# Fronts and w2 by Strassen's algorithm: joining copies of the fronts on ScalarE, the first summed tile of w2 in v's buffers, sums of h spread wider

## The chip, the cores and the metric

The kernel runs on one core of one Trainium2 chip. The metric is the device time of one execution in microseconds, the median of several runs; lower is better. The engines are called PE (matrix products), ACT (ScalarE), DVE (VectorE), POOL (GpSimd) and SP (SyncE, which here issues DMAs).

## The reference

A trunk of two layers works on 256 tokens (SEQ) of width 1024 (D_MODEL); the hidden width of a feed-forward part (FFN) is 2816 (D_FF). All of it is float32.

```python
def _swiglu(x, w1, w3, w2):
    return (jax.nn.silu(x @ w1) * (x @ w3)) @ w2

for l in range(DEPTH):                       # DEPTH = 2
    h = _swiglu(x, ffn_w1[l, 0], ffn_w3[l, 0], ffn_w2[l, 0])
    x = _layernorm(ALPHA * x + 0.5 * h, ln_g[l, 0], ln_b[l, 0])
    h = _mixer(x, l, ...)                    # gated unit and differential attention
    x = _layernorm(ALPHA * x + h, ln_g[l, 1], ln_b[l, 1])
    h = _swiglu(x, ffn_w1[l, 1], ffn_w3[l, 1], ffn_w2[l, 1])
    x = _layernorm(ALPHA * x + 0.5 * h, ln_g[l, 2], ln_b[l, 2])
```

The change concerns the four `_swiglu` calls. In order of time they are FFN 1 (0 to 189 us of the profiled execution), FFN 2 (421 to 607), FFN 3 (607 to 786) and FFN 4 (1018 to 1210); a mixer lies between FFN 1 and 2 and between FFN 3 and 4.

## The kernel before

**Products in three parts.** A float32 product is made of three faster ones: each operand is split into a high half and a low half, and PE adds hi·hi, lo·hi and hi·lo. Weights come from memory as tiles of 1 MB (`raw`, 128x2048; four buffers). For each half of such a tile, 128x1024, ACT copies the high half (`whi`) and DVE subtracts it from the tile, which gives the low half (`wlo`). Streamed tiles are split at L188 and L190 (`stream`), Strassen tiles at L234 and L236 (`split`). `hhi` and `hlo` are the halves of the hidden activations h. High and low halves have eight buffers each, so ACT and DVE can be at most a few tiles ahead of PE.

**The front of an FFN.** The tokens are two blocks t of 128. The columns of w1 and w3 are taken in five blocks of 512 (n = 0, 1, 2, 4 straight, by `rows_b`; n = 3 by Strassen's seven products, `seven`, one of which is fed in between two units of the others), and a rest of narrow columns by `gemm_a2`, whose low halves run at L289 and whose banks ACT empties at L290. For each block and t, Silu of one bank times the other gives a 128x512 tile, which must be turned (transposed) before it can be the left operand of w2. `transposed` does this in three steps: `parted` (L205) writes the two 16-bit halves of every number apart, a DMA on SP's queue transposes them (`moved`, L211; it stands behind the last load issued), and `joined` (L216) interleaves the halves again, with two copies for a tile. An FFN has ten such tiles, so 20 joining copies, and they run on POOL. The joined tile is then split into h_hi and h_lo.

**w2.** `gemm_seven` takes a 1024x1024 part of w2 by seven products P1 to P7 (L358) and the other columns and blocks straight (L387), some of these between two products (`between`). P1 uses r1 = w11, P2 w21, P3 r1 + r2 with r2 = w12, P4 r1 + r3 with r3 = w22, P5 r3, P6 r2 + w22, P7 r1 + w21 (the first two sums and their successors are made in place). `plus` (L342) adds two tiles on DVE; `gather` adds a tile from memory by an accumulating DMA that POOL issues. r2 and r3 are loaded into `spare`: two buffers that held x in the front. The left operands are blocks of h and four sums of them (`sums_of_h`, `strassen_sums`, L809). `ln.fold` (L584) adds a product's bank into the tokens.

**What sets the order.** PE's order is the order of the program text. The other engines are ordered by the priorities with which the text issues: `beside` starts a side task, which yields its delays in beats; a beat is the time of twelve matmuls. `front(n, wait)` gives the beats from the end of the product to the joining copies, through `turned`. Each engine then works its list strictly in order, and waits at the head of it. The buffers of tag "val" (called v's here: the mixer's value tiles) hold planes of blocks n = 0 and 2 in the fronts.

Of the kernel before, what the change touches and what calls it, by code (L numbers as in the profile page):

```python
# [11 lines left out]
F32 = mybir.dt.float32  # L12
# [4 lines left out]
AF = mybir.ActivationFunctionType  # L17
# [37 lines left out]
def trunk(ctx, tc, x, xT, w13a, w13b, w2, wb, wqk, wu, wg, wgr, wbr, wbrr, wo, gateb, gatebr, sgug, sgub, sguwT, sgubias, lam, diffg,  # L55
# [81 lines left out]
    def beside(task, delay):  # L137
        tasks.append([clock[0] + delay, task])
# [55 lines left out]
    def planes(v):  # L194
        return v.bitcast(U16).rearrange("p (w c) -> p w c", w=2)

    def numbers(v):
        return v.bitcast(U16).rearrange("p (c w) -> p w c", w=2)
# [14 lines left out]

    def joined(src, out, eng):
        for w in range(2):
            eng.tensor_copy(out=numbers(out)[:, w], in_=planes(src)[:, w])  # L216

    def transposed(src, out, via, lead, first, second, eng, to=None, by=None):

# [142 lines left out]
    def gemm_seven(src, xh, xl, sums, spare, ln, done):  # L362

        q = [[bank(), bank()], [side_bank(), bank()]]
        bx, bz = side_bank(), q[1][0]
        (w11, w21), (w12, w22) = ([s[:, o : o + CH] for o in (0, CH)] for s in src)

        def rest(c):
            for k in range(8, FT, 4):
                nk = min(4, FT - k)
                for j, piece in enumerate(stream(src[c][:, k * 512 : (k + nk) * 512], nk * 512)):
                    yield k + 2 * j, piece  # L380

        def rows(t, c, k0, piece, o=0, n=512):
            for j in range(2):
                k = k0 + j
                hi, lo = (w[:, j * 512 + o : j * 512 + o + n] for w in piece)
                for m, (y, x) in enumerate(((hi, xh), (lo, xh), (hi, xl))):
                    PE.matmul(q[c][t][:, :n] if o == 0 else more[:, :n], x(k, t), y,  # L387
                              start=k == 8 and m == 0 and (c, t) != (1, 0), stop=k == FT - 1 and m == 2, skip_group_check=True)
            beat(n / 1024)

        def block(t, k0):
            return tuple(lambda k, f=f: f(k0 + k, t) for f in (xh, xl))

        a11, a12, a22 = block(0, 0), block(0, 4), block(1, 4)
        first = rest(0)

        def between():
            k, piece = next(first)
            for t in range(NT):
                rows(t, 0, k, piece)  # L400

        r1 = fetch(w11)
        product(bx, a11, pieces(r1), True, False)
        ln.fold(0, 0, bx, ALU.add, True)
        between()
        product(q[0][0], a12, pieces(fetch(w21)), False, False)
        r2, r3 = (fetch(w, raw=v) for w, v in zip((w12, w22), spare))
        between()
        product(bz, sums[0], pieces(plus(r1, r2)), True, False)
        ln.fold(1, 1, bz, ALU.add, True)  # L410
        between()
        product(bx, sums[1], pieces(plus(r1, r3)), False, False)
        ln.fold(0, 1, bx, ALU.subtract, True)
        between()
        product(bz, sums[3], pieces(r3), False, False)
        between()
        product(bx, sums[2], pieces(gather(r2, w22)), False, False)
        ln.fold(1, 1, bx, ALU.subtract, False)
        between()
        product(bx, a22, pieces(gather(r1, w21)), False, True)  # L420
        ln.fold(1, 0, bx, ALU.add, True)
        between()
        for t in range(NT):
            done(t, q[0][t], 0, 512)
        held = list(rest(1))
        cuts = ((0, 512),), (((0, 256), (256, 256)) if ln.last else ((0, 512),))
        for t in range(NT):
            for o, n in cuts[t]:
                more = bank() if o else None
                for k, piece in held:  # L430
                    rows(t, 1, k, piece, o, n)
                done(t, (more if o else q[1][t])[:, :n], 512 + o, n)
# [289 lines left out]
    def ffn(l, f, i, norm, last=False):  # L722
# [42 lines left out]
        def turned(n, t, s, p, wait):  # L765
            lead = 3.5 if n == 0 and norm else 0
            to = slots("held", 2)[0] if n < 2 else p
            yield from transposed(s, p, s, lead, wait - lead, 0.6, G, to, A if n else G)
            yield 0.6
            if n < 2:  # L770
                held[n, t] = to
            if (n, t) != (0, 1):
                split(h_hi[2 * n + t], h_lo[2 * n + t], to, after=(silu[0], added[0]))
            if (n, t) == (1, 1):
                yield 1
                yield from sums_of_h()
# [3 lines left out]
        def sums_of_h():  # L780

            h11, h21, h12, h22 = (held[v] for v in ((0, 0), (0, 1), (1, 0), (1, 1)))
            made = [[h_hi[1], h_lo[1]]] + [[slots("sum", 2, F32R)[0] for _ in range(2)] for _ in range(2)]
            made.append([tmp.tile([P, 512], F32R, tag="side", name=name("sum"), bufs=4) for _ in range(2)])
            yield from strassen_sums(sums, made, h11, h21, h12, h22)

        def sums_of_x():

# [13 lines left out]
            made = [[home(v) for v in w] for w in (("main", "side"), ("side", "main"), ("main", "slot"), ("side", "slot"))]  # L802
            yield from strassen_sums(x_sums, made, t11, t21, t12, t22)

        def strassen_sums(to, made, v11, v21, v12, v22):
            to[:] = [tuple(lambda k, v=v: v[:, k * P : (k + 1) * P] for v in m) for m in made]
            for n, (out, a, b, op) in ((0, (v22, v21, v22, ALU.subtract)), (2, (v21, v11, v21, ALU.subtract)),
                                       (1, (v11, v22, v11, ALU.subtract)), (3, (v12, v12, v11, ALU.add))):
                V.tensor_tensor(out=out, in0=a, in1=b, op=op)  # L809
                if n in (2, 3):  # L810
                    yield 1
            for n, out in ((0, v22), (2, v21), (1, v11), (3, v12)):
                split(*made[n], out)
                yield 1

        def seven(src, x_sums):

# [23 lines left out]
            product(bz, x_sums[3], pieces(r3), False, True)  # L841
            V.tensor_tensor(out=v0, in0=bz, in1=v0, op=ALU.subtract)
            V.tensor_tensor(out=g0, in0=g0, in1=v0, op=ALU.mult)
            beside(turned(3, 0, g0, v0, 8.3), 0)
            yield
            product(bx, x_sums[2], pieces(r2), False, False)
            V.tensor_tensor(out=v1, in0=v1, in1=bx, op=ALU.subtract)
# [1 line left out]
            product(bx, x22, pieces(r1), False, True)  # L849
            A.activation(g1, bx, AF.Silu)  # L850
            V.tensor_tensor(out=g1, in0=g1, in1=v1, op=ALU.mult)
            beside(turned(3, 1, g1, v1, 6.3), 0)
            yield

        def w13(n):
# [1 line left out]

        x_sums = []
        if norm is None:
            gemm_first(w13(0), both_done(0, (10.3, 10.3)))  # L860
            beside(sums_of_x(), 1)
        else:
            gemm_b2(w13(0), xh, xl, both_done(0, (13.3, 10.3)), norm=norm)
            beside(sums_of_x(), 5)
        products, unit = seven(w13(3), x_sums), 0
        for n in (1, 2, NB - 1):
            ps = [[bank() for _ in range(2)] for _ in range(NT)]
            ready = front(n, (9.3, 8.3))
            for c in range(2):
                for m in range(2):  # L870
                    got = stream(w13(n)[m][:, c * CH : (c + 1) * CH])
# [8 lines left out]
        for j in range(FA, FT - 4, 2):  # L880
            for m, z in gemm_a2([w13a[l, f, j - FA + m] for m in range(2)], both, lambda m: t512("silu")):
# [1 line left out]
                silu[0] = A.activation(s, s, AF.Silu).ins  # L883
                V.tensor_tensor(out=s, in0=s, in1=z[:, T:], op=ALU.mult)
                split(*(v[-1][:, (j - FA + m) * T : (j - FA + m + 1) * T] for v in (h_hi, h_lo)), s)
        spare = [xs.tile([P, 4, 512], F32, tag="x", name=name("spare")).rearrange("p k c -> p (k c)") for _ in range(2)]
        ln = Norm(l, i, 2.0 * ALPHA, 4.0 * EPS, s[:, :1], last)

        def done(t, p, c, n):
# [396 lines left out]
```

## Time and profile before

| what | value |
|---|---|
| median of 3 runs | 1212.04 us (1209.83 to 1216.02) |
| the profiled execution | 1212.16 us, its span 1210.1 us |
| PE busy | 1187.0 us, 98% of the span |
| DVE busy | 1033.7 us, 85% |
| ACT busy | 798.6 us, 66% |
| POOL busy | 333.2 us, 28% |
| granted PE clock, mean | 0.999 |
| bytes moved | 281.39 MB, 233 GB/s |

A row of the timeline has the start and the duration in us, the engine, the line, the operation with output and inputs, and in brackets the idle time of the engine ahead of it and what ended that. The span is the profiled execution on the chip; the device time holds 2.06 us more.

### The profile page before, as it was taken

To read this page: it belongs to the slowest core of one execution; us is meant where nothing else is said; L and a number is where in the kernel's file an instruction comes from. 1 tells how busy PE (TensorE), PEld (TensorE's weight loads), DVE (VectorE), ACT (ScalarE), POOL (GpSimd) and SP (SyncE) were. 2 spreads that over 40 slices of the span, in tenths; PEclk is the share of its full clock that TensorE was granted. 3 is DMA by queue.
4 is the path that set the end of the run, shared out by engine and by line. 5 is a ranking of instruction groups with operands and counts; after the bars stand their busy time and mean duration, and the time that the engine had idled before them with its cause. 6 is when DMAs were issued, how large, how long until landed. Compare 5 with 4: busy or idle time off the path is not lost.

```text
span 1210.1 us, 16672 instructions
## 1 busy us (share of the span) xinstructions
PE 1187.0 (98%) x5771; PEld 993.5 (82%) x5771; DVE 1033.7 (85%) x1548; ACT 798.6 (66%) x1372; POOL 333.2 (28%) x414
## 2 busy tenths in 40 slices
PE   9998999999999999999999999999999999999998
PEld 7886788888888888887888887888888888888876
DVE  6799889797688988989898999888966989989895
ACT  6478558668955665775565765676788556667760
POOL 2243301246420222413022413003564012133120
PEclk9999999999999999999999999999999999999999
DMA  9996885767865659879759779676676754896880
GB/s 351 289 300 213 241 311 186 265 206 209 248 206 181 223 185 270 214 241 265 258 192 268 210 254 274 237 260 244 209 206 204 252 188 152 259 257 205 285 246 35
DMA packets 130084, 281.39 MB, mean 233 GB/s; under 512 B 89120, under 2 KB 90192, under 8 KB 104912
## 3 DMA queue, kind: packets, MB, share of 16 engines
q1 hardware_dynamic: 120816, 248.80, 62.3%
q0 software_dynamic: 8752, 31.00, 11.1%
q8 instruction: 45, 0.74, 0.2%
q10 hardware_dynamic: 432, 0.52, 0.1%
q14 instruction: 39, 0.32, 0.1%
HBM read 254.35 MB, written 1.05 MB: 211 GB/s over the span
## 4 chain that ended last, share of the span: by engine, by line
PE 84%; DVE 9%; DMA 5%; issue 2%; ACT 1%; SPq 0%; DVEq 0%; ACTq 0%
PE bank L270 42%; PE bank L282 15%; PE bank L289 7%; PE sbank L358 7%; PE bank L387 5%; PE sbank L387 3%; DVE wlo L190 2%; DMA spare<-in_w 2%; DVE wlo L236 2%; DVE raw L342 2%; DMA raw<-in_w 1%; PE bank L491 1%; DVE held L809 1%; PE sbank L945 1%; DVE hlo L236 1%
## 5 line engine op out<-in xcount | busy, mean ns | idle before, releaser
L190 DVE TENSOR_TENSOR wlo<-raw,whi 128x1024 fp32r<-128x1024 f32 (+1 forms) x374 | 428.2, 1176 | 43.0 <-ACT whi L188 30.3
L188 ACT ACTIVATE whi<-raw 128x1024 fp32r<-128x1024 f32 (+1 forms) x378 | 351.4, 959 | 148.3 <-PE bank L270 39.4
L270 PE MATMUL bank<-whi,x 128*128 128x512 f32 x1224 | 386.3, 390 | 0.0
L270 PEld LDWEIGHTS bank<-whi,x 128*128 128x128 f32 x1224 | 229.8, 188 | 47.5
L270 PE MATMUL bank<-wlo,x 128*128 128x512 f32 x612 | 239.0, 391 | 5.7 <-DVE wlo L190 5.6
L282 PE MATMUL bank<-x,whi 128*128 128x512 f32 x640 | 153.3, 391 | 0.0
L270 PEld LDWEIGHTS bank<-wlo,x 128*128 128x128 f32 x612 | 114.9, 188 | 31.7 <-DVE wlo L190 8.6
L282 PEld LDWEIGHTS bank<-x,whi 128*128 128x128 f32 x640 | 118.2, 188 | 23.8
L236 DVE TENSOR_TENSOR wlo<-raw,whi 128x1024 fp32r<-128x1024 f32 (+1 forms) x96 | 113.9, 1205 | 18.1 <-ACT whi L234 7.5
L234 ACT ACTIVATE whi<-raw 128x1024 fp32r<-128x1024 f32 (+1 forms) x96 | 92.9, 982 | 38.3 <-DVE raw L342 18.6
L289 PEld LDWEIGHTS bank<-x,wlo 128*128 128x128 f32 x640 | 81.4, 191 | 2.9
L289 PE MATMUL bank<-x,wlo 128*128 128x256 f32 x640 | 82.6, 283 | 0.0
L387 PE MATMUL bank<-whi,hhi 128*128 128x512 f32 (+1 forms) x182 | 68.2, 375 | 0.0
L387 PE MATMUL bank<-wlo,hhi 128*128 128x512 f32 (+1 forms) x182 | 67.9, 373 | 0.0
L387 PE MATMUL bank<-whi,hlo 128*128 128x512 f32 (+1 forms) x182 | 67.9, 373 | 0.0
L216 POOL COPY planes<-planes 128x512 uint16<-128x512 uint16 x32 | 40.7, 1329 | 55.2 <-DMA planes<-planes 30.4
L921 POOL TENSOR_TENSOR swap<-swap,sin_t 128x512 f32<-128x512 f32 x16 | 27.9, 1742 | 98.9 <-DMA swap<-z 80.5
L698 POOL COPY nvia<-ntwo 128x256 uint16<-128x256 uint16 x20 | 10.0, 548 | 153.0 <-DMA ntwo<-nvia 139.7
L290 ACT ACTIVATE r<-bank 128x256 f32<-128x256 f32 x96 | 34.8, 372 | 24.5 <-PE bank L289 24.5
L205 ACT ACTIVATE planes<-planes 128x512 uint16<-128x512 uint16 x48 | 27.4, 619 | 31.0 <-DVE planes L751 31.0
L216 POOL COPY held<-planes 128x512 uint16<-128x512 uint16 x32 | 46.2, 1645 | 5.6 <-DMA planes<-planes 5.6
L216 POOL COPY seven<-seven 128x512 uint16<-128x512 uint16 x16 | 20.9, 1353 | 77.4 <-DMA seven<-seven 38.2
(285 smaller groups left out, 2210.1 us busy)
## 6 DMA issues: line engine op xcount, KB each, us to landing
raw<-in_w13b SPq DMA_DIRECT2D x68, 1024.0 KB, 6.6
raw<-in_w SPq DMA_DIRECT2D x32, 1024.0 KB, 6.3
raw<-in_wb SPq DMA_DIRECT2D x16, 1024.0 KB, 6.7
raw<-in_wqk SPq DMA_DIRECT2D x16, 1024.0 KB, 5.9
r<-in_w13b SPq DMA_DIRECT2D x16, 512.0 KB, 8.0
raw<-in_w13a SPq DMA_DIRECT2D x8, 1024.0 KB, 4.8
spare<-in_w SPq DMA_DIRECT2D x8, 1024.0 KB, 6.8
raw<-in_wgr SPq DMA_DIRECT2D x8, 1024.0 KB, 5.2
```

The source lines that it names most:

```text
L188: A.activation(h, r, AF.Copy)
L190: eng.tensor_tensor(out=w, in0=r, in1=h.bitcast(F32), op=ALU.subtract)
L216: eng.tensor_copy(out=numbers(out)[:, w], in_=planes(src)[:, w])
L234: a = A.activation(hi, src, AF.Copy).ins
L236: return a, eng.tensor_tensor(out=lo, in0=src, in1=hi.bitcast(F32), op=ALU.subtract).ins
L270: PE.matmul(ps, xx, w, start=start and n == 0, stop=stop and n == 2)
L282: PE.matmul(b[-1], hi[:, k * P : (k + 1) * P], xc(k), start=k == 0, stop=False)
L289: PE.matmul(b[n][:, :T], lo[:, k * P : (k + 1) * P], xc(k)[:, :T], start=False, stop=k == KT - 1)
L290: emptied[0] = A.activation(r[:, s], b[n][:, T:], AF.Copy, scale=scale).ins
L358: PE.matmul(ps, x[o](k), y, start=start and k == n == 0, stop=stop and k == 3 and n == 2, skip_group_check=True)
L387: PE.matmul(q[c][t][:, :n] if o == 0 else more[:, :n], x(k, t), y, start=k == 8 and m == 0 and (c, t) != (1, 0), stop=k == FT - 1 and m == ...
L921: turned_by[0] = G.tensor_tensor(out=s3, in0=s3, in1=s, op=ALU.mult).ins
```

## The change

- **Joining copies.** `joined` can run on ACT, as activations with Copy, and the fronts' `turned` uses that: 80 copies leave POOL. The delay ahead of the copies grows from 0.6 to 2.6 beats behind the transposing DMA, and the beats ahead of that DMA, given to `front` and to the two tiles of `seven`, shrink by 2 or 2.3, so the DMA is issued earlier and the copies come at about the same beat. For block n = 4 the beats ahead of the DMA stay, and its copies come two beats later.
- **First summed tile of w2.** r2 goes into two buffers of tag "val", r3 into one x buffer. r2 is loaded and added to r1 before P1's matmuls; r2's gather moves to right behind P2, ahead of the load of r3, and r1's gather to right behind P4.
- **Sums of h.** The steps of `strassen_sums` for h are 1.5 beats apart and not 1; those for x stay at 1.

```diff
@@ -213,7 +213,11 @@
 
     def joined(src, out, eng):
         for w in range(2):
-            eng.tensor_copy(out=numbers(out)[:, w], in_=planes(src)[:, w])
+            o, i = numbers(out)[:, w], planes(src)[:, w]
+            if eng is A:
+                A.activation(o, i, AF.Copy)
+            else:
+                eng.tensor_copy(out=o, in_=i)
 
     def transposed(src, out, via, lead, first, second, eng, to=None, by=None):
 
@@ -400,24 +404,29 @@
                 rows(t, 0, k, piece)
 
         r1 = fetch(w11)
-        product(bx, a11, pieces(r1), True, False)
+        p1 = pieces(r1)
+        r2 = fetch(w12, raw=spare[0])
+        plus(r1, r2)
+        product(bx, a11, p1, True, False)
         ln.fold(0, 0, bx, ALU.add, True)
         between()
         product(q[0][0], a12, pieces(fetch(w21)), False, False)
-        r2, r3 = (fetch(w, raw=v) for w, v in zip((w12, w22), spare))
+        gather(r2, w22)
+        r3 = fetch(w22, raw=spare[1])
         between()
-        product(bz, sums[0], pieces(plus(r1, r2)), True, False)
+        product(bz, sums[0], pieces(r1), True, False)
         ln.fold(1, 1, bz, ALU.add, True)
         between()
         product(bx, sums[1], pieces(plus(r1, r3)), False, False)
         ln.fold(0, 1, bx, ALU.subtract, True)
+        gather(r1, w21)
         between()
         product(bz, sums[3], pieces(r3), False, False)
         between()
-        product(bx, sums[2], pieces(gather(r2, w22)), False, False)
+        product(bx, sums[2], pieces(r2), False, False)
         ln.fold(1, 1, bx, ALU.subtract, False)
         between()
-        product(bx, a22, pieces(gather(r1, w21)), False, True)
+        product(bx, a22, pieces(r1), False, True)
         ln.fold(1, 0, bx, ALU.add, True)
         between()
         for t in range(NT):
@@ -765,7 +774,7 @@
         def turned(n, t, s, p, wait):
             lead = 3.5 if n == 0 and norm else 0
             to = slots("held", 2)[0] if n < 2 else p
-            yield from transposed(s, p, s, lead, wait - lead, 0.6, G, to, A if n else G)
+            yield from transposed(s, p, s, lead, wait - lead, 2.6, A, to, A if n else G)
             yield 0.6
             if n < 2:
                 held[n, t] = to
@@ -782,7 +791,7 @@
             h11, h21, h12, h22 = (held[v] for v in ((0, 0), (0, 1), (1, 0), (1, 1)))
             made = [[h_hi[1], h_lo[1]]] + [[slots("sum", 2, F32R)[0] for _ in range(2)] for _ in range(2)]
             made.append([tmp.tile([P, 512], F32R, tag="side", name=name("sum"), bufs=4) for _ in range(2)])
-            yield from strassen_sums(sums, made, h11, h21, h12, h22)
+            yield from strassen_sums(sums, made, h11, h21, h12, h22, 1.5)
 
         def sums_of_x():
 
@@ -802,16 +811,16 @@
             made = [[home(v) for v in w] for w in (("main", "side"), ("side", "main"), ("main", "slot"), ("side", "slot"))]
             yield from strassen_sums(x_sums, made, t11, t21, t12, t22)
 
-        def strassen_sums(to, made, v11, v21, v12, v22):
+        def strassen_sums(to, made, v11, v21, v12, v22, apart=1):
             to[:] = [tuple(lambda k, v=v: v[:, k * P : (k + 1) * P] for v in m) for m in made]
             for n, (out, a, b, op) in ((0, (v22, v21, v22, ALU.subtract)), (2, (v21, v11, v21, ALU.subtract)),
                                        (1, (v11, v22, v11, ALU.subtract)), (3, (v12, v12, v11, ALU.add))):
                 V.tensor_tensor(out=out, in0=a, in1=b, op=op)
                 if n in (2, 3):
-                    yield 1
+                    yield apart
             for n, out in ((0, v22), (2, v21), (1, v11), (3, v12)):
                 split(*made[n], out)
-                yield 1
+                yield apart
 
         def seven(src, x_sums):
 
@@ -841,7 +850,7 @@
             product(bz, x_sums[3], pieces(r3), False, True)
             V.tensor_tensor(out=v0, in0=bz, in1=v0, op=ALU.subtract)
             V.tensor_tensor(out=g0, in0=g0, in1=v0, op=ALU.mult)
-            beside(turned(3, 0, g0, v0, 8.3), 0)
+            beside(turned(3, 0, g0, v0, 6.3), 0)
             yield
             product(bx, x_sums[2], pieces(r2), False, False)
             V.tensor_tensor(out=v1, in0=v1, in1=bx, op=ALU.subtract)
@@ -849,7 +858,7 @@
             product(bx, x22, pieces(r1), False, True)
             A.activation(g1, bx, AF.Silu)
             V.tensor_tensor(out=g1, in0=g1, in1=v1, op=ALU.mult)
-            beside(turned(3, 1, g1, v1, 6.3), 0)
+            beside(turned(3, 1, g1, v1, 4), 0)
             yield
 
         def w13(n):
@@ -857,15 +866,15 @@
 
         x_sums = []
         if norm is None:
-            gemm_first(w13(0), both_done(0, (10.3, 10.3)))
+            gemm_first(w13(0), both_done(0, (8.3, 8.3)))
             beside(sums_of_x(), 1)
         else:
-            gemm_b2(w13(0), xh, xl, both_done(0, (13.3, 10.3)), norm=norm)
+            gemm_b2(w13(0), xh, xl, both_done(0, (11.3, 8.3)), norm=norm)
             beside(sums_of_x(), 5)
         products, unit = seven(w13(3), x_sums), 0
         for n in (1, 2, NB - 1):
             ps = [[bank() for _ in range(2)] for _ in range(NT)]
-            ready = front(n, (9.3, 8.3))
+            ready = front(n, (7.3, 6.3) if n < NB - 1 else (9.3, 8.3))
             for c in range(2):
                 for m in range(2):
                     got = stream(w13(n)[m][:, c * CH : (c + 1) * CH])
@@ -883,7 +892,8 @@
                 silu[0] = A.activation(s, s, AF.Silu).ins
                 V.tensor_tensor(out=s, in0=s, in1=z[:, T:], op=ALU.mult)
                 split(*(v[-1][:, (j - FA + m) * T : (j - FA + m + 1) * T] for v in (h_hi, h_lo)), s)
-        spare = [xs.tile([P, 4, 512], F32, tag="x", name=name("spare")).rearrange("p k c -> p (k c)") for _ in range(2)]
+        spare = [[act.tile([P, D], F32, tag="val", name=name("spare"), bufs=2) for _ in range(2)],
+                 xs.tile([P, 4, 512], F32, tag="x", name=name("spare")).rearrange("p k c -> p (k c)")]
         ln = Norm(l, i, 2.0 * ALPHA, 4.0 * EPS, s[:, :1], last)
 
         def done(t, p, c, n):
```

PE's order is the same before and after. Three places show what moves elsewhere, all in FFN 2. Line numbers of the changed kernel are larger: L188 and L190 stay, L216 becomes L218 where ACT copies, L234 and L236 become L238 and L240, L290 becomes L294, and L809 becomes L818.

The first is ACT from the end of the front into w2; `raw_5372` (`raw_5377` after) is r1, to which first r2 and then r3 is added, and `planes_5173` and `planes_5189` (`planes_5176` and `planes_5190`) are the two tiles of block n = 4. Before:

```order
L290 ACTIVATE r_5300<-bank_5250 128x256
L290 ACTIVATE r_5300<-bank_5263 128x256
...
L234 ACTIVATE hhi_4301<-seven_4579 128x512
L234 ACTIVATE hhi_4304<-silu_5328 128x256
L234 ACTIVATE whi_5457<-raw_5372 128x1024
L234 ACTIVATE whi_5461<-raw_5372 128x1024
L188 ACTIVATE whi_5482<-raw_5480 128x1024
L188 ACTIVATE whi_5486<-raw_5480 128x1024
L234 ACTIVATE hhi_4302<-planes_5173 128x512
L234 ACTIVATE whi_5508<-raw_5372 128x1024
L234 ACTIVATE hhi_4303<-planes_5189 128x512
L234 ACTIVATE whi_5512<-raw_5372 128x1024
```

After:

```order
L238 ACTIVATE whi_5463<-raw_5377 128x1024
L238 ACTIVATE whi_5467<-raw_5377 128x1024
L294 ACTIVATE r_5303<-bank_5252 128x256
L294 ACTIVATE r_5303<-bank_5266 128x256
...
L188 ACTIVATE whi_5488<-raw_5486 128x1024
L238 ACTIVATE hhi_4306<-silu_5332 128x256
L188 ACTIVATE whi_5492<-raw_5486 128x1024
L218 ACTIVATE planes_5176<-planes_5176 128x512 x2
L218 ACTIVATE planes_5190<-planes_5190 128x512 x2
L238 ACTIVATE hhi_4304<-planes_5176 128x512
L238 ACTIVATE whi_5510<-raw_5377 128x1024
L238 ACTIVATE hhi_4305<-planes_5190 128x512
```

The high halves of r1 + r2 now stand ahead of the copies that empty the banks (L290, now L294); behind them the joining copies of both tiles stand ahead of the high halves of r1 + r3.

The second is DVE at the sums of h; `held` are the joined tiles of blocks n = 0 and 1. Before:

```order
L842 TENSOR_TENSOR seven_4578<-sbank_4575,seven_4578 128x512
L809 TENSOR_TENSOR held_4781<-held_4555,held_4781 128x512
L843 TENSOR_TENSOR seven_4577<-seven_4577,seven_4578 128x512
L809 TENSOR_TENSOR held_4555<-held_4473,held_4555 128x512
L236 TENSOR_TENSOR hlo_4306<-held_4781,hhi_4295 128x512
L809 TENSOR_TENSOR held_4473<-held_4781,held_4473 128x512
L190 TENSOR_TENSOR wlo_5090<-raw_5087,whi_5089 128x1024
L809 TENSOR_TENSOR held_4755<-held_4755,held_4473 128x512
L190 TENSOR_TENSOR wlo_5094<-raw_5087,whi_5093 128x1024
L236 TENSOR_TENSOR sum_5045<-held_4555,sum_5044 128x512
```

After:

```order
L851 TENSOR_TENSOR seven_4580<-sbank_4577,seven_4580 128x512
L818 TENSOR_TENSOR held_4784<-held_4557,held_4784 128x512
L852 TENSOR_TENSOR seven_4579<-seven_4579,seven_4580 128x512
L818 TENSOR_TENSOR held_4557<-held_4475,held_4557 128x512
L190 TENSOR_TENSOR wlo_5090<-raw_5087,whi_5089 128x1024
L818 TENSOR_TENSOR held_4475<-held_4784,held_4475 128x512
L190 TENSOR_TENSOR wlo_5094<-raw_5087,whi_5093 128x1024
L818 TENSOR_TENSOR held_4759<-held_4759,held_4475 128x512
L240 TENSOR_TENSOR hlo_4308<-held_4784,hhi_4297 128x512
```

The four sums (L809, now L818) are the same and as many, with two streamed low halves (L190) brought in ahead of the last of them.

The third is SP's queue at the loads of r2 and r3. Before:

```order
L166 DMA raw_5419<-in_w 128x2048
L166 DMA raw_5480<-in_w 128x2048
L166 DMA raw_5565<-in_w 128x2048
L166 DMA spare_5355<-in_w 128x2048
L166 DMA spare_5356<-in_w 128x2048
L211 DMA_TRANSPOSE planes_5173<-planes_5173 128x8x128
L211 DMA_TRANSPOSE planes_5189<-planes_5189 128x8x128
```

After:

```order
L166 DMA raw_5426<-in_w 128x2048
L166 DMA raw_5486<-in_w 128x2048
L164 DMA spare_5359<-in_w 128x1024
L164 DMA spare_5360<-in_w 128x1024
L166 DMA raw_5573<-in_w 128x2048
L166 DMA spare_5361<-in_w 128x2048
L211 DMA_TRANSPOSE planes_5176<-planes_5176 128x8x128
L211 DMA_TRANSPOSE planes_5190<-planes_5190 128x8x128
```

r2 is now two loads of half the size and goes ahead of a tile of the rest of w2; r3 alone still goes into x's buffer. The transposes behind them are the same.

## The prediction

> **What bounds the kernel now.** FFN 1 to 4 are the four half-step FFNs in order of time, P1 to P7 the seven products of a Strassen stage. I read the page first, then the waits of PE alone.
>
> ```profile
> span 1210.1 us, 16672 instructions
> PE 1187.0 (98%) x5771; PEld 993.5 (82%) x5771; DVE 1033.7 (85%) x1548; ACT 798.6 (66%) x1372; POOL 333.2 (28%) x414
> PE sbank L358 <- DVE wlo L236: 8.5, 5, 2.6
> PE bank L270 <- DVE wlo L190: 5.6, 5, 3.3
> ```
>
> PE is busy but for 1210.1 - 1187.0 = 23.1 us, and ten waits for a low half (wlo, made by DVE) hold 14.1 of these. The change leaves PE's order as it is, so PE's idle time is all it can win. Next I took the timeline of PE around each wait; the bracket is the idle time before the row.
>
> ```profile
> 94.01 0.50 PE L358 MATMUL sbank<-wlo,xhs 128*128 128x512 f32 x1 [1.04 <-DVE wlo L236]
> 98.99 0.49 PE L270 MATMUL bank<-wlo,x 128*128 128x512 f32 x1 [3.32 <-DVE wlo L190]
> 479.30 0.50 PE L270 MATMUL bank<-wlo,x 128*128 128x512 f32 x1 [0.21 <-DVE wlo L190]
> 516.39 0.50 PE L270 MATMUL bank<-wlo,x 128*128 128x512 f32 x1 [1.11 <-DVE wlo L190]
> 696.67 0.50 PE L270 MATMUL bank<-wlo,x 128*128 128x512 f32 x1 [0.49 <-DVE wlo L190]
> 1111.84 0.49 PE L270 MATMUL bank<-wlo,x 128*128 128x512 f32 x1 [0.52 <-DVE wlo L190]
> 145.39 0.39 PE L358 MATMUL sbank<-whi,sum 128*128 128x512 f32 x1
> 147.03 0.50 PE L358 MATMUL sbank<-wlo,sum 128*128 128x512 f32 x1 [1.26 <-DVE wlo L236]
> 147.37 0.40 PE L358 MATMUL sbank<-whi,sum 128*128 128x512 f32 x1
> 564.44 0.50 PE L358 MATMUL sbank<-wlo,sum 128*128 128x512 f32 x1 [2.64 <-DVE wlo L236]
> 568.65 0.40 PE L387 MATMUL bank<-whi,hhi 128*128 128x512 f32 x1
> 743.94 0.50 PE L358 MATMUL sbank<-wlo,sum 128*128 128x512 f32 x1 [1.86 <-DVE wlo L236]
> 760.60 0.47 PE L358 MATMUL sbank<-whi,hhi 128*128 128x512 f32 x1 [0.27 <-DVE xtok L584]
> 1158.98 0.50 PE L358 MATMUL sbank<-wlo,sum 128*128 128x512 f32 x1 [1.71 <-DVE wlo L236]
> 1176.32 0.47 PE L358 MATMUL sbank<-whi,hhi 128*128 128x512 f32 x1 [0.91 <-DVE xtok L584]
> 152.90 2.72 PE sbank L358 x12
> ```
>
> Six stalls lie in the fronts (6.69 us), four at P4 of w2 (147, 564, 744, 1159: 7.47), two at P7 of w2 (1.18): 15.34. A stall costs more than its idle: a matmul's step is 2.72 / 12 = 0.227 us (last row, of the chain), and from 145.39 to 147.37 pass 1.98 us for two steps of 0.45, so 1.53 are lost for 1.26 idle, 0.27 more. At 564.44 eleven matmuls take 4.21 us where 2.50 do, 1.71 more; PE's clock fell there:
>
> ```profile
> 541.00:607.00 66.00, 63.36 (x289) 52.60 (x288) 57.20 (x79) 39.11 (x56) 11.14 (x12) 0.97 0.82 251
> ```
>
> (stretches; the column before the last two is the granted clock, 0.97). The Trainium skill (TensorE: Matmul & The Clock Gate, Part 1) has the clock halve only after an idle window of about 3.4 us; here 2.64 us did it and 3.32 us (98.99) did not, so the trace differs. By that rule FFN 2 would give back about 1.6 less. The ceiling is 15.34 + 12 x 0.27 + 1.6 = 20.2 us.
>
> **The copies go from POOL to ACT.**
>
> ```profile
> L216 POOL COPY held<-planes 128x512 uint16<-128x512 uint16 x32 | 46.2, 1645 | 5.6 <-DMA planes<-planes 5.6
> L216 POOL COPY planes<-planes 128x512 uint16<-128x512 uint16 x32 | 40.7, 1329 | 55.2 <-DMA planes<-planes 30.4 <-DVE hlo L236 23.7 <-ACT whi L188 1.0
> L216 POOL COPY seven<-seven 128x512 uint16<-128x512 uint16 x16 | 20.9, 1353 | 77.4 <-DMA seven<-seven 38.2 <-DVE wlo L236 36.9 <-DVE wlo L190 2.3
> L205 ACT ACTIVATE planes<-planes 128x512 uint16<-128x512 uint16 x48 | 27.4, 619 | 31.0 <-DVE planes L751 31.0
> L993 ACT ACTIVATE aT<-d 128x512 uint16<-128x512 uint16 x16 | 11.3, 777 | 0.0
> 507.87 0.68 DVE L843 TENSOR_TENSOR seven<-seven,seven 128x512 f32<-128x512 f32 x1
> 508.47 1.20 DVE L809 TENSOR_TENSOR held<-held,held 128x512 f32<-128x512 f32 x1
> 71.87 5.36 DVE L190 TENSOR_TENSOR wlo<-raw,whi 128x1024 fp32r<-128x1024 f32 x1
> 44.39 2.36 DVE L190 TENSOR_TENSOR wlo<-raw,whi 128x1024 fp32r<-128x1024 f32 x2 [1.04 <-ACT whi L188]
> 72.04 5.80 POOL L216 COPY held<-planes 128x512 uint16<-128x512 uint16 x6
> ```
>
> 80 copies, 20 in each FFN, leave POOL. On ACT one costs between 0.619 (the same size, the halves read apart) and 0.777 us (written apart, as here); I take 0.777: 15.5 us an FFN, ACT at 861 of 1210. What DVE gets back: an operation of 0.68 us takes 1.20 beside a copy, and one of 2.36 / 2 = 1.18 takes 5.36 beside six: 0.5 to 0.7 a copy, at most 20 x 0.7 = 14 us an FFN, at least 0 where copy and DVE do not meet. I take 20 x 0.5 = 10. The Trainium skill (SBUF — State Buffer, Who interferes with whom) calls this an exclusive lock, in which a DVE operation with two inputs in SBUF stands still until the copy has ended; by that DVE would get back whole copies, 107.8 / 4 = 27 us an FFN, and the end would be the third rival's. The trace shows a part of a copy only.
>
> With 10 us in hand, and with two lows moved ahead of the sums of h by the wider spread (no work added), DVE is ahead of PE by more than the longest front stall, 3.32 + 0.27 = 3.59 us. Five of the six go: 6.69 - 0.21 + 5 x 0.27 = 7.8 us. The one at 479.30 follows a load and stays:
>
> ```profile
> 476.88 1.23 DVE L342 TENSOR_TENSOR raw<-raw,r 128x1024 f32<-128x1024 f32 x1 [4.70 <-DMA r<-in_w13b]
> 494.48 3.43 POOL L216 COPY held<-planes 128x512 uint16<-128x512 uint16 x2 [3.29 <-DMA planes<-planes]
> ```
>
> New is that ACT waits for transposes, with high halves (whi) queued behind. The worst place I see is FFN 2: the transpose lands at 494.4, POOL joins there, 3.29 us after it had run out of work, and on ACT these two copies (2 x 0.78) now stand ahead of the second whi<-r of the unit, whose low comes as much later; the slack that this eats is part of the 10 us. On SP a transpose passes one load in the front, which is the later by the transpose's time on the queue; PE's next need of that load is several rows off. For both I take 1 us back (0 to 4).
>
> **First summed tile of w2 in v's buffers.**
>
> ```profile
> 544.77 0.81 SPq L166 DMA_DIRECT2D spare<-in_w  x2
> 550.62 2.36 DVE L342 TENSOR_TENSOR raw<-raw,spare 128x1024 f32<-128x1024 f32 x2 [1.86 <-DMA spare<-in_w]
> 559.65 2.44 POOL L216 COPY planes<-planes 128x512 uint16<-128x512 uint16 x2 [0.84 <-DMA planes<-planes]
> 542.38 0.38 ACT L290 ACTIVATE r<-bank 128x256 f32<-128x256 f32 x1 [0.49 <-PE bank L289]
> 547.81 0.39 PE L387 MATMUL bank<-whi,hhi 128*128 128x512 f32 x1
> 535.27 1.80 DVE L236 TENSOR_TENSOR hlo<-planes,hhi 128x512 fp32r<-128x512 f32 x2
> spare<-in_w SPq DMA_DIRECT2D x8, 1024.0 KB, 6.8
> ```
>
> Before, both summed tiles load at 544.77, when x's buffers come free; DVE waits 1.86 us, adds r1 + r2 (2.36), and only then gets to r1 + r3, on which P4 waits. Now r1 + r2 is added ahead of L290, and P4's sum starts up to 1.86 + 2.36 = 4.2 us earlier and with no copy on POOL beside it. P4's stalls go: 7.47 + 4 x 0.27 + 1.6 = 10.2 us. What is late next, in FFN 2's clock:
> - ACT has both planes copies ahead of the whi of r1 + r3. The second transpose landed at 559.6; with one load ahead of it instead of two it should come some us earlier, but if not, whi starts after two copies and one hhi (0.6, taken like the 0.619), at 559.6 + 2 x 0.78 + 0.6 = 561.8; with whi put at 1.1 and the low at 1.18, P4, whose low is due at 564.44 - 2.64 = 561.8, waits for it until about 564.1. 0 to 2.5 us an FFN; I take 0.5, 2 in all.
> - L290, which empties the banks that PE's rows at 547.81 write, now stands behind whi of r1 + r2 on ACT. v's buffers come free at 537.1 (535.27 + 1.80); 1 us put for the issue and 6.8 for the load give 544.9, add and whi 2.2 (1.18 and about 1): L290 at 547.1, the bank free some 0.8 later, at 547.9. 0 to 3 us an FFN; I take 0.5, 2 in all.
> - P7 waits for the fold L584, which now has one more low (1.18) ahead of it. Its two stalls stay, and FFN 2 gets one of up to 1 us.
>
> The gathers come earlier on POOL, where no joining copy stands ahead of them any more, and their products, P6 and P7, keep their places: nothing to gain or lose there, as PE shows no wait for a gather's tile.
>
> **Sum.** 7.8 + 10.2 - 1 - 2 - 2 - 1 = 12.0 us. The profiled execution took 1212.16 us (2.06 beside its span), 0.12 from the median 1212.04, which changes nothing: **1200 us**.
>
> **Rivals.**
> - *Handed over*: the transposes land no earlier and P4's stall stays in another name, 2.5 us an FFN. Gain 12.0 - 4 x 2 = 4, or less: about 1208. For it: 559.65. Against: 1 MB less ahead.
> - *Slower*: r2's second half lands late, and L290 and with it the banks. Each us past 545 is a us of PE in each FFN; from 548 it has eaten the gain, at 550 the sum is 1200 + 4 x 5 = 1220. For it: v is freed only behind the second seven copies, themselves waiting for a transpose, and the loads at 494 took long. Against: at 537 the queue is light.
> - *All of it*: the ceiling without the 479.30 and P7 stalls, 18 us: 1194.
> - That the copies do not run on ACT cannot be: the form is L993's.
>
> **Chances.** Forecast 0.60 (own range 1196 to 1206), handed over 0.16, slower 0.14, all 0.10. Within 0.5% (6 us, about what this kernel's runs tell apart) lie the second and a little of the first. Faster by more 0.67, within 0.19, slower 0.14. Range 1192 to 1215: it holds the first three cases but the slower one's upper part.
>
> **What would show it.** Right: no joining copy on POOL, DVE's L809 at 0.68 us, ACT's copies near 0.78, PE without idle at P4 and in FFN 1's front. Wrong: a bracket on PE naming L290's bank or a whi behind a planes copy, ACT waiting for planes<-planes over 2 us an FFN, or copies well over 0.8 us.

## The result and the profile after

The change makes no difference that these runs can tell: 1210.86 us (median of 12, 1206.38 to 1214.55) against 1210.51 us (12, 1205.46 to 1216.02) before, ratio 1.000 (95% interval 0.998 to 1.002). The forecast was 12 us faster.

There are two profiled executions of the changed kernel, and neither is typical alone: one took 1206.38 us, the shortest of its 12, the other 1218.27, the second longest of 12 in a later series (median 1211.24). They bracket the usual execution, so both are read. The waits of PE in the first:

```profile
span 1204.6 us, 16667 instructions
PE 1184.8 (98%) x5771; PEld 993.6 (82%) x5771; DVE 998.5 (83%) x1548; ACT 842.4 (70%) x1452; POOL 227.7 (19%) x334
PE sbank L362 <- DVE xtok L593: 6.9, 4, 3.1
PE bank L274 <- DVE wlo L190: 1.7, 2, 1.1
PE sbank L362 <- DVE wlo L240: 1.6, 1, 1.6
```

and in the second (L362 is the products' line, L358 before; L593 the fold, L584 before; L274 the fronts', L270 before):

```profile
PE sbank L362 <- DVE xtok L593: 13.5, 4, 4.0
PE sbank L362 <- DVE bc L559: 1.5, 4, 0.5
PE sbank L362 <- DVE wlo L240: 1.0, 1, 1.0
PE bank L274 <- DVE wlo L190: 0.3, 1, 0.3
```

(The columns are total, times, longest.) The ten waits for a low half, 14.1 us before, are down to 3.3 and 1.3: what the change aimed at, it got. One wait has grown in their place. P7, the last product of w2, now waits once in each FFN for the fold of P6: two waits and 1.2 us before, four waits and 6.9 or 13.5 us now. And PE's clock falls behind a long one. FFN 2 of the second profile, PE's rows around P7's first matmul:

```profile
577.12 0.39 PE L391 MATMUL bank<-whi,hlo 128*128 128x512 f32 x1
581.47 0.77 PE L362 MATMUL sbank<-whi,hhi 128*128 128x512 f32 x1 [3.96 <-DVE xtok L593]
582.04 0.63 PE L362 MATMUL sbank<-wlo,hhi 128*128 128x512 f32 x1
...
585.88 0.63 PE L362 MATMUL sbank<-wlo,hhi 128*128 128x512 f32 x1
```

Ten steps take 585.88 - 581.47 = 4.41 us, where ten steps of 0.227 take 2.27: 2.1 us on top of the wait of 3.96. The chain that ends there, on POOL, ACT and DVE of the same execution:

```profile
561.24 0.85 POOL L341 DMA_DIRECT2D raw<-in_w  x1 [18.20 <-DVE bc L559]
561.78 0.86 POOL L560 DMA_DIRECT2D bc<-in_lng  x1
562.71 0.85 POOL L341 DMA_DIRECT2D raw<-in_w  x1
566.75 1.04 ACT L238 ACTIVATE whi<-raw 128x1024 fp32r<-128x1024 f32 x1
573.87 1.06 ACT L238 ACTIVATE whi<-raw 128x1024 fp32r<-128x1024 f32 x1 [6.08 <-DMA raw<-in_w]
574.84 4.83 ACT L188 ACTIVATE whi<-raw 128x1024 fp32r<-128x1024 f32 x5
574.96 1.23 DVE L240 TENSOR_TENSOR wlo<-raw,whi 128x1024 fp32r<-128x1024 f32 x1 [2.75 <-ACT whi L238]
576.11 4.62 DVE L190 TENSOR_TENSOR wlo<-raw,whi 128x1024 fp32r<-128x1024 f32 x4
580.65 0.68 DVE L593 SCALAR_TENSOR_TENSOR xtok<-xtok,sbank 128x512 f32<-128x512 f32 x1
```

POOL issues the two halves of r1's gather (L341) at 561.24 and 562.71, and between them the load of one of the norm's vectors (bc, L560). The second half lands only at 573.9, 11.2 us after its issue; ACT stands at its head for 6.08 us; DVE makes its low at 574.96, then four streamed lows (4.62 us) that nothing needs yet, and only then the fold. P7 writes the bank that the fold reads, so it waits for that.

### The profile page after: what moved, and what is told of

Read it like the earlier page. It is cut to its first block, busy times and chain, and to the rows that moved or that the text cites. A ratio compares the mean times of both kernels' runs of the same rounds, so it can differ in the third digit from the quotient of the medians.

```text
span 1204.6 us, 16667 instructions
## 1 busy us (share of the span) xinstructions
PE 1184.8 (98%) x5771; PEld 993.6 (82%) x5771; DVE 998.5 (83%) x1548; ACT 842.4 (70%) x1452; POOL 227.7 (19%) x334
## 4 chain that ended last, share of the span: by engine, by line
PE 80%; issue 7%; DMA 7%; DVE 3%; ACT 1%; POOL 1%; SPq 0%; POOLq 0%; DVEq 0%; ACTq 0%
PE bank L274 42%; PE bank L286 13%; PE sbank L362 7%; PE bank L293 6%; PE bank L391 4%; DMA raw<-in_w 3%; PE sbank L391 3%; DVE wlo L190 2%; DMA r<-in_w13b 2%; PE bank L500 1%; PE sbank L955 1%; DMA raw<-in_w13b 1%; ACT whi L238 1%; PE sbank L1011 1%; PE sbank L1129 1%
## 5 line engine op out<-in xcount | busy, mean ns | idle before, releaser
L190 DVE TENSOR_TENSOR wlo<-raw,whi 128x1024 fp32r<-128x1024 f32 (+1 forms) x374 | 413.8, 1135 | 59.0 <-ACT whi L188 45.9
L188 ACT ACTIVATE whi<-raw 128x1024 fp32r<-128x1024 f32 (+1 forms) x378 | 350.0, 958 | 129.0 <-PE bank L274 38.0
L274 PE MATMUL bank<-whi,x 128*128 128x512 f32 x1224 | 386.3, 390 | 0.0
L274 PEld LDWEIGHTS bank<-whi,x 128*128 128x128 f32 x1224 | 229.8, 188 | 47.4
L274 PE MATMUL bank<-wlo,x 128*128 128x512 f32 x612 | 238.7, 390 | 1.8 <-DVE wlo L190 1.7
L274 PEld LDWEIGHTS bank<-wlo,x 128*128 128x128 f32 x612 | 114.9, 188 | 26.9 <-DVE wlo L190 3.5
L240 DVE TENSOR_TENSOR wlo<-raw,whi 128x1024 fp32r<-128x1024 f32 (+1 forms) x96 | 109.4, 1153 | 13.2 <-ACT whi L238 9.7
L238 ACT ACTIVATE whi<-raw 128x1024 fp32r<-128x1024 f32 (+1 forms) x96 | 92.4, 980 | 25.4 <-DMA raw<-in_w 15.3
L341 POOL DMA_DIRECT2D spare<-in_w x8 | 6.8, 851 | 204.5 <-DVE raw L346 203.5
L294 ACT ACTIVATE r<-bank 128x256 f32<-128x256 f32 x96 | 34.5, 371 | 15.6 <-PE bank L293 15.5
L362 PE MATMUL sbank<-whi,xhs 128*128 128x512 f32 x128 | 42.0, 389 | 0.0
L391 PEld LDWEIGHTS bank<-whi,hlo 128*128 128x128 f32 x182 | 34.3, 188 | 6.1
L391 PEld LDWEIGHTS bank<-wlo,hhi 128*128 128x128 f32 x182 | 34.3, 188 | 6.0
```

Of the source, the lines that this page charges most:

```text
L188: A.activation(h, r, AF.Copy)
L190: eng.tensor_tensor(out=w, in0=r, in1=h.bitcast(F32), op=ALU.subtract)
L238: a = A.activation(hi, src, AF.Copy).ins
L240: return a, eng.tensor_tensor(out=lo, in0=src, in1=hi.bitcast(F32), op=ALU.subtract).ins
L274: PE.matmul(ps, xx, w, start=start and n == 0, stop=stop and n == 2)
L294: emptied[0] = A.activation(r[:, s], b[n][:, T:], AF.Copy, scale=scale).ins
```

## Experiments

The theory: P4's stall was handed on to P7, because the chain from r1's gather over ScalarE to DVE's list (low, four lows, fold) has a pace of its own that P4's stall had hidden. The rivals: the copies on ScalarE give back what DVE wins; or the first profile hides something else, such as clock.

**after_again**: the changed kernel unedited.

> The changed kernel once more, for a second profile and more times. Its first profile (1206.38 us) is the shortest of 12 executions with a median of 1210.86, at a granted clock of 0.998 where the others show 0.994 to 0.997. If P7's wait for the fold of P6 is what gives the gain back, a usual execution (about 1211) shows P7's four waits again, about 7 us or more in all, and more places where the clock falls. If the copies on ScalarE give it back, it shows new waits in the fronts instead, behind high halves that stand behind a joining copy, 4 us or more above the first profile. Ratio to before 0.998 to 1.002.

Measured: 1211.24 us (12 runs), ratio 1.0004 (0.9981 to 1.0027). The profile is the second one above: P7's waits are doubled, and no wait for a high half behind a copy appears in the fronts. The median granted clock of its executions is 0.9955, that of the runs before beside it 0.998.

**joins_only**: the kernel before, with

```diff
...
-            yield from transposed(s, p, s, lead, wait - lead, 0.6, G, to, A if n else G)
+            yield from transposed(s, p, s, lead, wait - lead, 2.6, A, to, A if n else G)
...
```

and the shorter beats of `front` and `seven`.

> Only the joining copies go to ScalarE, with their retuned delays; w2 and the spread of the sums as before. If P7's fold is the cause, the fronts keep their gain (about 3 us of PE's waits) and P4 of w2 waits as before (about 7 us in four waits): ratio about 0.997. If the copies give back what they win, 1.000 to 1.004.

Measured: 1207.48 us, ratio 0.9965 (0.9942 to 0.9988), as the theory has it. The copies by themselves are a gain, so the rival that blames them falls. P7's wait grows even here, from 1.2 to 3.4:

```profile
PE sbank L362 <- DVE wlo L240: 4.3, 4, 1.1
PE sbank L362 <- DVE xtok L588: 3.4, 4, 1.0
```

**w2_only**: the changed kernel without the copies' move (with the longer beats of before) and without the spread.

```diff
...
-            yield from transposed(s, p, s, lead, wait - lead, 2.6, A, to, A if n else G)
+            yield from transposed(s, p, s, lead, wait - lead, 0.6, G, to, A if n else G)
...
-            yield from strassen_sums(sums, made, h11, h21, h12, h22, 1.5)
+            yield from strassen_sums(sums, made, h11, h21, h12, h22)
...
```

> Only the loads, sums and gathers of w2 are moved; joining copies on POOL, spread 1 beat. If P7's fold is the cause, P4's waits go (7 us down to about 1) and P7's grow from 1.2 to about 6 us: ratio 1.000 within 0.002. If the reordering were good and only the copies were bad, 0.994 or less.

Measured: 1230.09 us, ratio 1.0141 (1.0112 to 1.0169), granted clock 0.990. The place was right and the size far off: w2's reordering alone costs 20 us. Waits of PE:

```profile
PE sbank L358 <- DVE xtok L589: 19.4, 4, 5.6
PE bank L270 <- DVE wlo L190: 3.9, 5, 1.3
PE sbank L358 <- DVE wlo L236: 3.9, 2, 3.6
```

Against the second profile of the changed kernel that is 5.9 us more at P7 and 7.8 - 1.3 = 6.5 more at low halves, which come with the copies back on POOL; the clock (medians 0.990 against 0.9955, of some 1210 us) makes 6.7 more. These come to the 19 us between the two medians, in part by luck: the two profiled executions lie only 15.1 us apart. The gather is later here too: in FFN 2 POOL issues its halves at 569.17 and 572.59, with the loads of both of the norm's vectors between them. The parts are not additive: the copies' move and the spread are worth 19 us here, the copies alone 3 on the kernel before. That P4's stall hides less of DVE's lateness here is the likely reason, argued and not shown.

**fold_first**: the changed kernel; the streamed lows of the last rows are ordered behind P6's fold.

```diff
...
-        ln.fold(1, 1, bx, ALU.subtract, False)
+        folded = ln.fold(1, 1, bx, ALU.subtract, False)
...
-                for j, piece in enumerate(stream(src[c][:, k * 512 : (k + nk) * 512], nk * 512)):
+                for j, piece in enumerate(stream(src[c][:, k * 512 : (k + nk) * 512], nk * 512, after=[folded if c == 0 or k < 16 else None] * 2)):
...
```

> The changed kernel, with the fold of P6 (L593) ordered ahead of the four streamed low halves on DVE that stood before it; the streamed lows of the last rows come later instead. If P7's fold is the cause, P7 waits at most 1 us in all and the kernel is 6 to 9 us faster than the changed one: ratio to before 0.992 to 0.995. If something else gives the gain back (the copies, the clock, the loads), it stays within 2 us of the changed kernel: 0.998 to 1.002.

Measured: 1194.69 us (4 runs, 1193.08 to 1195.61), ratio 0.9858 (0.9834 to 0.9881): 16 us faster than the changed kernel's 1211.24 by one order on one engine. That is more than expected; the expectation went by the first profile's waits. ACT, DVE and PE in FFN 2:

```profile
567.13 1.06 ACT L238 ACTIVATE whi<-raw 128x1024 fp32r<-128x1024 f32 x1 [4.89 <-DMA raw<-in_w]
568.22 1.23 DVE L240 TENSOR_TENSOR wlo<-raw,whi 128x1024 fp32r<-128x1024 f32 x1 [1.56 <-ACT whi L238]
569.36 0.68 DVE L593 SCALAR_TENSOR_TENSOR xtok<-xtok,sbank 128x512 f32<-128x512 f32 x1
569.96 5.76 DVE L190 TENSOR_TENSOR wlo<-raw,whi 128x1024 fp32r<-128x1024 f32 x5
571.78 0.39 PE L362 MATMUL sbank<-whi,hhi 128*128 128x512 f32 x1
```

The gather is still late (ACT waits 4.89), but the fold stands right behind P7's own low and ends at 569.36 + 0.68 = 570.04, 1.7 us before P7 needs it, and P7 (last row) starts without a bracket.

**fold_first_again**: the same kernel.

> The version with the fold first once more, for more times: 1193 to 1196, ratio 0.985 to 0.988, P7 without a wait and a granted clock of 0.999 or more in all executions.

Measured: 1195.23 us (5 runs, 1194.61 to 1203.11), ratio 0.9884 (0.9855 to 0.9913). P7 is without a wait, and the clock 0.999 or more in each run. The profile, of the run of 1198.21, has one long wait elsewhere (2.6 us for a low half in FFN 1's front, at 96). What made the run of 1203.11 is not on record. This is the fastest version tried.

**fold_after_two**: as fold_first, but two of the four lows stay ahead of the fold.

```diff
...
-nk * 512, after=[folded if c == 0 or k < 16 else None] * 2)):
+nk * 512, after=[None, folded] if c and k == 8 else [folded if c and k == 12 else None] * 2)):
...
```

> The changed kernel, with the fold of P6 behind two of the four streamed lows instead of all. Two lows are 2.3 us. Theory (the wait is the place of the fold in DVE's list, and PE's clock falls only behind a long wait): P7 waits about 13.5 - 4 x 2.3 = 4 us in all, 0.5 to 2 each, without a fall of the clock: 1194.7 + 4 + 4 x 0.27 = 1200, ratio 0.990 to 0.994. If the clock falls behind the short waits too, 1206, ratio 0.997. If the fold's place doesn't matter by itself, 1195 or 1211.

Measured: 1199.25 us (10 runs, 1194.76 to 1208.66), ratio 0.990 (0.9871 to 0.9929), median clock 0.9995. P7 waits 1.8 us in its profile, where 4 were expected. The dose answers: 1195 with no low ahead of the fold, 1199 with two, 1211 with four. The first step alone isn't settled, since the interval overlaps that of fold_first_again; the second is clear. That the second pair costs more fits the clock: P7's waits are at most 1.0 us with two lows, with no fall behind them, and 3 to 4 us with four in the changed kernel's second profile.

**no_gather**: the changed kernel without r1's gather.

```diff
-        gather(r1, w21)
+        step()
```

> The changed kernel, with r1's gather left out (w21 is not added to r1, so P7 multiplies by another matrix; all instructions of the engines stay, 8 accumulating DMAs of 512 KB go). Theory, the gather starts the chain: ScalarE stands up to 6 us at the high half of the gathered tile, the four streamed highs and lows stand behind that, and the fold behind them. Then P7 waits under 2 us in all and the kernel comes to 1195 to 1199, ratio 0.987 to 0.990. Rival, the four lows alone are too much for DVE there: P7 waits 6 us or more in all, 1204 to 1211, ratio 0.995 to 1.001.

Measured: 1202.01 us (6 runs, 1195.23 to 1210.96), ratio 0.9936 (0.9899 to 0.9972): between the two expectations. Its profile, of the shortest run, shows P7 waiting 3.4 us in three FFNs with DVE working without a pause, here in FFN 1:

```profile
149.24 2.35 DVE L240 TENSOR_TENSOR wlo<-spare,whi 128x1024 fp32r<-128x1024 f32 x2
151.51 2.35 DVE L240 TENSOR_TENSOR wlo<-raw,whi 128x1024 fp32r<-128x1024 f32 x2
153.78 4.62 DVE L190 TENSOR_TENSOR wlo<-raw,whi 128x1024 fp32r<-128x1024 f32 x4
158.32 0.68 DVE L593 SCALAR_TENSOR_TENSOR xtok<-xtok,sbank 128x512 f32<-128x512 f32 x1
```

So the gather is the larger part of the lateness, and in this execution the four lows by themselves make about a microsecond in three of the four FFNs.

**bc_later**: the changed kernel; the loads of the norm's vectors are issued behind both halves of the gather.

```diff
-            self.g, self.b = bc_load(lng[l, i], after), bc_load(lnb[l, i], after)
+            if after is not None:
+                self.load(l, i, after)
...
         gather(r1, w21)
+        ln.load(*ln.at, ln.y[1][:, :1])
```

> The changed kernel, with the two loads of the norm's vectors (bc, 512 KB each, on POOL's queue) moved behind both halves of r1's gather; before, the first of them was issued between the halves. Theory, the second half is late because it stands behind that load on the queue (issued at 562.7, landed at 573.9; the first half took about 5.5): it lands 4 to 6 us sooner, P7 waits 2 to 5 us in all instead of 13.5, and the kernel comes to 1198 to 1204, ratio 0.989 to 0.995. Rival, the second half is late because the weight loads share the engines of the DMA: it lands no more than 1 us sooner, 1208 to 1212, ratio 0.998 to 1.002.

Measured: 1203.52 us, ratio 0.9937 (0.9916 to 0.9958), as the theory has it; P7 waits 4.4 us in its profile. POOL and ACT in FFN 2:

```profile
558.01 0.85 POOL L341 DMA_DIRECT2D raw<-in_w  x1 [0.62 <-DVE bc L560]
558.56 0.85 POOL L561 DMA_DIRECT2D bc<-in_lng  x1
564.43 1.06 ACT L238 ACTIVATE whi<-raw 128x1024 fp32r<-128x1024 f32 x1 [1.32 <-DMA raw<-in_w]
```

The second half (issued at 558.01) now lands 6.4 us behind its issue instead of 11.2. Wherever ACT stood waiting for it, it is 6.4 to 6.9 us here and 10.1 to 11.2 in the two profiles of the changed kernel, so the load that stood ahead of it on POOL's queue made 3 to 5 of these. FFN 4 keeps P7's longest wait of this run, 2.23 us: ACT scales the norm's vector there, ahead of r1's high halves, and now waits 4.90 us for its load (bc, at 1153.50).

**before_fold_first**, **joins_fold** and **w2_fold**: the edit of fold_first on the kernel before, on joins_only and on w2_only.

> The kernel before, with only the fold of P6 ahead of the streamed lows. P4 still waits for its low half, 7 us in all, so the fold has time: only P7's 1.2 us go, with what a usual execution has more: 1 to 3 us, ratio 0.997 to 0.999. If the fold by itself were the gain, whatever P4 does, 1200 or less, ratio 0.992.

> The kernel before with the joining copies on ScalarE and the fold of P6 ahead of the streamed lows; w2's loads and sums as before. P7's waits (3.4 us in the run with the copies alone) go, P4's (4.3 us for a low half, 2.1 for a high) stay: 1207.5 - 3.4 - 1 = 1203, ratio 0.992 to 0.996. If the fold is worth nothing without w2's reordering, 1207, ratio 0.997.

> The kernel before with w2's loads, sums and gathers moved and the fold of P6 ahead of the streamed lows; joining copies on POOL, spread 1. Of the 1230 of w2's reordering alone, P7's 19.4 us of waits and four falls of the clock (1.6 each) go: 1230 - 19.4 - 6.4 = 1204, ratio 0.993 to 0.998. If copies on POOL hold the rest, new waits at P7's own low halves take the place: 1212 or more, ratio above 1.001.

Measured, with their counterparts (ratios to before):

| | fold behind the lows | fold first |
|---|---|---|
| kernel before | 1 | 0.9991 (0.9971 to 1.0011), 1209.74 us |
| copies on ScalarE | 0.9965 | 0.9919 (0.9882 to 0.9955), 1201.53 us |
| w2 reordered | 1.0141 | 0.9976 (0.9953 to 1.0000), 1208.39 us |
| all of the change | 1.000 | 0.9858 and 0.9884, 1194.69 and 1195.23 us |

The fold's place is worth nothing that can be told as long as P4 holds PE up (first row), about 0.5% with the copies (the two intervals overlap), and 1.2 to 1.7% where w2 is reordered. That is a hidden wait: its price appears when the wait ahead of it goes. In the third row P7 is not free of waits even with the fold first: three of 3.6 us in all, which a high half on ACT ended.

**fold_first_spread1**: fold_first with `strassen_sums(sums, made, h11, h21, h12, h22, 1)`.

> The changed kernel with the fold of P6 ahead of the streamed lows, and the sums of h spread by 1 beat as before. If the wider spread moves only DVE's order where DVE has time: ratio 0.985 to 0.988, the same as with it. If the spread carries the front's gain, PE waits for low halves at the sums of h again (2 us or more in the fronts) and the ratio is 0.988 or more.

Measured: 1200.88 us, ratio 0.9906 (0.9876 to 0.9936), against 0.9884 (0.9855 to 0.9913) for fold_first_again beside it. The intervals overlap, and PE waits for low halves in the fronts for 2.6 us here and 2.8 in the other's profile; whether the wider spread gains is not settled.

## Why the prediction was wrong

**Right: what the copies cost and free.** On ACT a copy takes 0.767 to 0.774 us (0.777 taken), and DVE's sums of h run at 0.684 us (0.68 named), both in the first profile:

```profile
L218 ACT ACTIVATE planes<-planes 128x512 uint16<-128x512 uint16 x32 | 21.3, 767 | 18.5 <-DMA planes<-planes 18.5
L218 ACT ACTIVATE seven<-seven 128x512 uint16<-128x512 uint16 x16 | 11.4, 774 | 0.0
L818 DVE TENSOR_TENSOR held<-held,held 128x512 f32<-128x512 f32 x16 | 10.9, 684 | 0.0
```

DVE's busy time fell by 1033.7 - 998.5 = 35.2 us (40 taken). ACT's came to 842.4 us, less than the 861 of the prediction. The fronts' stalls, 6.69 us, are 3.3 and 1.3 in the two profiles. With the fold out of the way the copies (without the wider spread) are worth 0.9991 - 0.9919 = 0.7% or 9 us, with intervals of 2 to 4 us each way (7.8 - 1 was the sum).

**Right: P4.** Its four stalls, 7.47 us, are down to 0.6 us in the first profile and 1.5 in the second, where they stand as the wait for bc (L559), a copy just ahead of P4's second low on DVE.

**Right: no stall at L290.** The load of r2 in FFN 2 of the second profile, on DVE:

```profile
539.19 2.47 DVE L346 TENSOR_TENSOR raw<-raw,spare 128x1024 f32<-128x1024 f32 x2 [1.77 <-DMA spare<-in_w]
```

r1 + r2 was added from 539.19 on, nearly 6 us ahead of the 545 from which the slower rival counted, and PE shows no wait for an emptied bank. That rival fell, and so did the way in which the gain was to be handed over, by P4's stall itself.

**Without harm, though named as a sign against it:** ACT waits 18.5 us for the transposes (the bracket of the first row above), over 4 an FFN. PE sees little of it: the lows of P4 stand behind these copies, and P4's waits are the 0.6 and 1.5 us above, near the 2 us that the sum took off for them.

**Wrong: the third point under w2, "P7 waits for the fold", priced at 1 us in all.** It measured 6.9 and 13.5 us of waiting in the two profiles, 5.7 and 12.3 more than before, and falls of the clock behind the waits of 3 us and more. The step counted what the change adds ahead of the fold (one low) and not what it takes away ahead of P7: P4's stall. A wait was removed, but the readiness of what comes next was not compared with the earlier time at which it would now be wanted. The trace of before held most of the answer, on DVE and PE in FFN 2:

```profile
573.99 2.36 DVE L236 TENSOR_TENSOR wlo<-raw,whi 128x1024 fp32r<-128x1024 f32 x2
576.26 3.49 DVE L190 TENSOR_TENSOR wlo<-raw,whi 128x1024 fp32r<-128x1024 f32 x3
579.77 0.69 DVE L584 SCALAR_TENSOR_TENSOR xtok<-xtok,sbank 128x512 f32<-128x512 f32 x1
582.29 0.39 PE L358 MATMUL sbank<-whi,hhi 128*128 128x512 f32 x1
```

The fold ended at 579.77 + 0.69 = 580.46, and P7 started at 582.29: a margin of 1.8 us. Taking P4's 2.64 + 0.27 + 1.6 = 4.5 us away brings P7 to 577.8, 2.7 us before that end. In FFN 3 and 4 there was no margin at all (P7 already waited 0.27 and 0.91), so P4's 1.86 + 0.27 and 1.71 + 0.27 pass through whole and make waits of 2.4 and 2.9 us. Given back are 2.7 + 2.1 + 2.0 = 6.8 us, and if PE's clock falls behind each of the three as it did at 564.44, some 1.6 us each, 4.8 more. By this estimate, made after the fact, 11.6 of the forecast 12 go, but that it comes so near is in part luck. It takes the fold's end as it stood, and in FFN 2 that holds: 580.46 before, 579.36 + 0.68 = 580.04 and 580.65 + 0.68 = 581.33 in the two profiles. But the first profile's waits in FFN 2 to 4 were 0.96, 1.38 and 1.50 us, too short for a fall, and the second's 3.96, 3.04 and 3.28. And FFN 1 is left out: P7 waited 3.06 and 3.22 us there, twice what P4's 1.26 + 0.27 can hand on, so the rest has another source: the added low (1.18), the late gather, or PE's earlier arrival once the front's stalls are gone. The record doesn't part these.

**The "handed over" rival** came nearest in time (1208), and had the handing over right but the place wrong and the price too small: P4's stall under another name, 2 us an FFN, where it was a later product that waited, in the second profile longer than P4 had.

**Also missing:** the gather. The text costed its move on POOL at nothing because PE showed no wait for its tile. But a load of the norm's vectors came to stand between its halves, where before it had been issued ahead of both (563.82, halves at 564.68 and 565.81 in FFN 2). bc_later prices that at 0.6%. Issued 3 us earlier than before, the second half reached ACT hardly earlier: at 572.59 and 573.87 in the two profiles, against 573.97.

## What to carry to other kernels

When a change removes a stall, everything behind it on that engine is wanted earlier by as much: take the margin of the next few waits from the trace (when was the input ready, when was it used) and subtract. A gain passes only as far as the first margin that is smaller, so look at what stands ahead of that input in its engine's strict order; here the instruction that P7 waited for stood behind four that nobody needed yet, and moving it ahead gained 16 us where the change alone had gained nothing. And one profile of a kernel whose runs spread by 1% is one draw: take a second before reading small differences from it.

## What the hardware showed

**When the clock falls.** In the 14 traces of this case, from 20 to 1180 us, the ten matmuls of 128x512 behind a wait take 2.4 to 2.8 us after gaps of 0.8 to 2.0 us (start to start, less one step), apart from those into which a second wait or an earlier fall reaches. After gaps of 2.4 to 5.2 us they take 3.6 to 4.8 us in 12 of 14 cases; the 4.8 holds a second wait. The shortest that did it, in FFN 4 of bc_later:

```profile
1160.57 0.39 PE L391 MATMUL bank<-whi,hlo 128*128 128x512 f32 x1
1163.19 0.77 PE L362 MATMUL sbank<-whi,hhi 128*128 128x512 f32 x1 [2.23 <-DVE xtok L599]
1163.75 0.63 PE L362 MATMUL sbank<-wlo,hhi 128*128 128x512 f32 x1
1164.18 0.63 PE L362 MATMUL sbank<-whi,hlo 128*128 128x512 f32 x1
```

Steps of 0.56 and 0.43 us instead of 0.227 follow a wait of 2.23. The two behind which it did not fall lie at 96 us (fold_first_again, 2.6 us) and 99 us (before, 3.3 us), in FFN 1. The Trainium skill (TensorE: Matmul & The Clock Gate, Part 1) puts the fall behind an idle window of about 3.4 us that runs free of the program. Seven of the 12 waits here that made it fall were shorter, so the traces differ from that figure; that waits of 2.6 and 3.3 us were spared, where 2.23 was not, would suit a window that runs free. The ten matmuls behind the wait of 2.23 took 3.84 us instead of 2.27, so it cost nearly twice its length. That this is what spread the changed kernel's times is argued from their clocks (0.992 to 0.999), not shown.

**Queue of POOL.** An accumulating load of 512 KB landed 6.4 to 6.9 us after its issue with nothing ahead of it but the other half (bc_later, FFN 1 to 3), and 10.1 to 11.2 us with another 512 KB load between them (after and after_again, wherever ACT waited for it).
